# Fewer helpers on GpSimd, and 512 moving columns in four linears of a two-block transformer kernel

## The chip, the cores and the metric

The kernel runs on one core of a Trainium2 chip. TensorE (PE) does matrix products, VectorE (DVE) and ScalarE (ACT) elementwise work, GpSimd (POOL) a little of the same, and SyncE (SP) issues most DMAs. The metric is the device time of one execution in microseconds, as a median of several runs.

## The reference

Two transformer blocks on 256 tokens of width 1024, everything in float32, about 150 MB of weights. Cut to the linears and norms that matter here:

```python
# first block; 16 meta tokens in front, so 272 rows
proj  = rms_norm(h, g0) @ w_in                      # 1024 -> 5128
mixed = (sigmoid(g_a) * (o_a @ w_o_fox) + sigmoid(g_b) * (o_b @ w_o_sb)) @ w_out
h = h + rms_norm(mixed, g1)
u = causal_depthwise_conv(rms_norm(h, g2) @ w_up)   # 1024 -> 5632, 3 taps
ffn = (gelu(u_gate) * u_val) @ w_down               # 2816 -> 1024
h = h + rms_norm(ffn, g3)
# second block, 256 tokens
proj = rms_norm(x, g_mix) @ w_in_2                  # 1024 -> 8192: qa ka va qr kr vr gr ga gr
x = x + (sigmoid(ga) * (ya @ w_branch_diff) + sigmoid(gr) * (yr @ w_branch_ret)) @ w_out_2
x = x + square(relu(rms_norm(x, g_mlp) @ w_ff1)) @ w_ff2
x = x + sigmoid(rms_norm(x, g_ple) @ w_ple_gate) * (p @ w_ple)
return rms_norm(x, g_final)
```

`o_a` and `o_b` are two attentions of the first block; `ya` (differential attention) and `yr` (retention) belong to the second.

## The kernel before

**Precision.** Every large product is made of three matmuls. A weight slab `w` (up to 1024 rows by 256 columns, as 8 chunks of 128 rows) is split into a high part `whi`, which ScalarE writes by a copy (`Weights.split_unit`, L87), and a low part `wlo` = `w` - `whi`, by a subtraction (`Weights.finish`, L96). Activations have high and low parts too (`xh` and `xl`, `fh` and `fl`). The three products are high by high, high by low and low by high.

**Weights.** The object `ws` walks a list of slabs, `plan`, in the order in which the program uses them. SyncE loads half slabs ("units", 128 partitions by 1024 elements, tile `raw`, five buffers). `ws.start(n)` splits the next unit or units on ScalarE, at most two slabs ahead; `ws.finish()` issues the subtractions that belong to them and the next loads; `ws.next()` hands out the next slab and splits it on the spot if that has not been done. Before, `finish` puts a subtraction on GpSimd in two cases: when it is called as `finish(True)` (in the residual of the first block, at the end of w_down, and in the first va wave), and as every fourth one while `ws.share` is 4, that is, during w_up. That makes 17 of 284.

**Two forms of linear.** `feat_tile` (L320 to L323) holds the weights still and moves the activations: the result has features on the partitions. `token_tile` (L333 to L336) holds 128 tokens still and moves the weights: the result has tokens on the partitions. Four linears have the second form: w_down, va and vr of the second block, and ple_gate. They take slabs of 256 columns and 256 moving columns.

**Order of the work.** The program is written in the order in which each engine executes it. Between two tiles of a linear stands `period()`: it starts the next units' high parts on ScalarE, lets the evacuation of the tile before go on a step (`side.evac`), runs a step of side work such as attention (`side.tick`), and ends with the low parts (`ws.finish`). Evacuations are generators, one step at each `yield`. A linear may begin with a wave: three tiles share each chunk, while the chunk's activation is still being made by `make(k)`.

**The places touched.** In w_up, `ev_conv` evacuates a tile of 258 columns: VectorE multiplies it by the reciprocal root (`ur`, L302), applies the taps of the convolution (`cv`, two instructions at L308, one on ScalarE), and after each second tile makes the gated product. In w_down, `ev_down` copies a tile to `rawt` and sums its squares (`ssf`); the last tile's rows are scaled with a reciprocal root (`down_rstd`, `down_scale`), transposed (`turn_raw`) and added to the residual `R`, from which ScalarE makes `xh` and VectorE `xl` for the second block's first linear, va. This is called the join below. Its square sums (`squares`, `mix_sums`) are folded from eight chunks to two on GpSimd and summed by TensorE against a column of ones. `ev_mix` makes the `xl` of the gated mix, six of its eight low parts on GpSimd.

Of the kernel before, what the change touches and what calls it, by code (L numbers as in the profile page):

```python
# [27 lines left out]
DOWN = ((0, 6), (6, 8), (14, 8))  # L28
# [141 lines left out]
def two_blocks_kernel(  # L170
# [42 lines left out]
    for c in range(0, D, 256):  # L213
        for k, nk in DOWN:
            cols(w_down[0], c, 256, k, nk)
    all_cols(w_in_2, 2 * D, D)
# [3 lines left out]
    all_cols(w_in_2, 3 * D, 5 * D)  # L220
# [7 lines left out]
    all_cols(w_ple_gate[0], 0, D)  # L228
# [188 lines left out]

    def tp_tile(tag, n):
# [6 lines left out]
    def period(gen=None, finish=True):  # L425
        ws.start()
# [4 lines left out]
        if finish:  # L431
# [8 lines left out]

    def token_tiles(slabs, X):
        for _ in range(slabs):
            W = ws.next()
            for t in range(2):
                yield lambda ps, k, nk, part=None, W=W, t=t: token_tile(
                    ps, X, W, k, k, t, k == 0, k == nk - 1)

    def linear(tiles, nk, evac, wave=0, make=None, sums=None, after=None, settle=9, hold=0, pump=(2, 4)):
# [31 lines left out]
        for f in tiles:  # L480
# [6 lines left out]
            j += 1  # L487

# [348 lines left out]
    def ev_mix(ps, j):  # L837
# [5 lines left out]
        (G if j < 6 else V).tensor_tensor(xl[:, j, 0:NQ], t, f32(xh[:, j, 0:NQ]), ALU.subtract)  # L843
# [40 lines left out]
    def residual(sums, after, toks, off, n, gout, gnext, fill):  # L884
# [5 lines left out]
        ws.finish(True)  # L890
# [21 lines left out]
        def make(k):  # L912
# [11 lines left out]
            if k in (5, 7):  # L924
# [95 lines left out]
    for c in range(4):  # L1020
        pss = [mm(), mm()]
        for k0, nk in DOWN:
            W = ws.next()
# [4 lines left out]
            for t in range(2):  # L1028
                for k in range(nk):
                    token_tile(pss[t], FX, W, k0 + k, k, t, k0 + k == 0, k0 + k == KF1 - 1)  # L1030
                if c < 3 or not last:
                    period(ev_down(pss[t], c, t) if last else None)
                    continue
                side.flush()
                next(ev_down(pss[t], c, t))
                if t == 0:
                    down_scale(0, down_rstd(0))
# [45 lines left out]
    def ev_va(ps, c, t):  # L1083
        A.activation(va[:, t, c * 256:(c + 1) * 256], ps[:, 0:256], AF.Identity, scale=r3[:, t:t + 1])
# [3 lines left out]
    wave = [[mm(), mm()], [mm(), mm()]]  # L1088
# [3 lines left out]
    for t in range(2):  # L1092
# [3 lines left out]
        for k in range(KD):  # L1096
# [49 lines left out]
    def ev_tokens(dst):  # L1146
        def go(ps, j):
            c, t = divmod(j, 2)
            A.activation(dst[:, t, c * 256:(c + 1) * 256], ps[:, 0:256], AF.Identity,
                         scale=r3[:, t:t + 1])  # L1150
# [136 lines left out]
    W = None  # L1287
    for j in range(4):
        c, t = divmod(j + 4, 2)
        W = W if t else ws.next()  # L1290
        ps = mm()
        for k in range(KD):
            token_tile(ps, X3, W, k, k, t, k == 0, k == KD - 1)
        if j == 0:
            ws.start()
            ws.finish()
            mix_sums(1)
            mix_rstd(1)
# [211 lines left out]
```

## Time and profile before

| | before |
|---|---|
| median of 3 runs | 939.78 us (938.76, 939.78, 940.41) |
| the profiled execution | 937.62 us; its span 935.8 us |
| TensorE busy | 909.7 us, 97%, 7457 matmuls |
| weight loads (PEld) busy | 884.8 us, 95% |
| VectorE busy | 647.0 us, 69% |
| ScalarE busy | 522.5 us, 56% |
| GpSimd busy | 88.1 us, 9%, 75 instructions |
| DMA | 154.73 MB, mean 165 GB/s |

The span is the stretch from the first to the last instruction in the trace; the execution's own time is 1.8 us longer. Stages, by the trace: w_up runs from about 240 to 362 us, w_down from 362 to 431 us, the join and the first va wave from 431 to about 459 us, ple_gate at the end. PEclk is the clock granted to TensorE as a share of full speed.

### The profile page before, as it was taken

Reading aid. Unit: us, or ns where it says so; the run is one execution under the profiler, and the core shown is the slowest. Engines: PE = TensorE matmul, PEld = TensorE weight load, DVE = VectorE, ACT = ScalarE, POOL = GpSimd, SP = SyncE. Lnnn points to the kernel's source line nnn. Section 1 sums busy time; section 2 is a strip of 40 time slices with the busy share of each in tenths; the row PEclk is TensorE's granted clock in tenths of the full one; section 3 lists DMA queues with packets and bytes.
Section 4 is the critical chain, followed back from the end, with each engine's and each line's share of the span. In section 5 each row is a group of like instructions: output and inputs, shape, how many; then the busy total and the mean of one; then the engine's idle time right before and its main releaser. Section 6 shows DMA issues by size and latency. Waiting matters only on the chain.

```text
span 935.8 us, 18318 instructions
## 1 busy us (share of the span) xinstructions
PE 909.7 (97%) x7457; PEld 884.8 (95%) x7457; DVE 647.0 (69%) x1150; ACT 522.5 (56%) x948; POOL 88.1 (9%) x75
## 2 busy tenths in 40 slices
PE   8999999999999999999899999999999999999996
PEld 5999989998999999898899999999999999999996
DVE  5667666667899999536667765577787666655546
ACT  5535566656666666546556564446645566544435
POOL 5021100032422222003200000000000000000000
PEclk8999999999999999999999999999999999999998
DMA  8554343664355555663555465455465666565631
GB/s 268 169 147 137 112 130 100 202 212 136 113 164 179 180 173 163 208 197 113 180 164 153 147 195 167 139 166 191 143 200 179 185 197 189 172 203 180 197 120 45
DMA packets 149715, 154.73 MB, mean 165 GB/s; under 512 B 5260, under 2 KB 145808, under 8 KB 149632
## 3 DMA queue, kind: packets, MB, share of 16 engines
q1 hardware_dynamic: 147904, 149.56, 51.7%
q0 software_dynamic: 1376, 3.36, 1.1%
q8 instruction: 58, 0.95, 0.4%
q10 hardware_dynamic: 352, 0.66, 0.2%
q14 instruction: 25, 0.20, 0.1%
HBM read 152.50 MB, written 1.05 MB: 164 GB/s over the span
## 4 chain that ended last, share of the span: by engine, by line
PE 77%; DVE 16%; ACT 3%; issue 2%; DMA 1%; POOL 0%; SPq 0%; DVEq 0%; ACTq 0%
PE mm L320 19%; PE mm L323 19%; PE mm L321 19%; DVE cv L308 5%; DVE wlo L96 4%; PE mm L336 4%; PE mm L333 4%; PE mm L334 4%; DVE ur L302 2%; DVE cv L302 1%; PE at L678 1%; DMA raw<-in_w_in_dram 1%; PE at L1164 1%; ACT whi L87 1%; DVE u L989 1%
## 5 line engine op out<-in xcount | busy, mean ns | idle before, releaser
L96 DVE TENSOR_TENSOR wlo<-raw,whi 128x1024 fp32r<-128x1024 f32 (+1 forms) x267 | 324.4, 1223 | 98.5 <-ACT whi L87 97.8
L87 ACT ACTIVATE whi<-raw 128x1024 fp32r<-128x1024 f32 (+1 forms) x284 | 292.0, 1047 | 172.5 <-PE mm L323 87.9
L323 PE MATMUL mm<-xl,whi 128*128 128x258 f32 (+2 forms) x1256 | 351.1, 283 | 1.3 <-DVE xl L308 1.3
L320 PE MATMUL mm<-xh,whi 128*128 128x258 f32 (+3 forms) x1192 | 341.5, 287 | 1.9 <-ACT xh L542 1.9
L321 PE MATMUL mm<-xh,wlo 128*128 128x258 f32 (+3 forms) x1192 | 337.0, 283 | 0.3 <-DVE wlo L96 0.3
L323 PEld LDWEIGHTS mm<-xl,whi 128*128 128x128 f32 x1256 | 235.4, 189 | 2.0 <-DVE xl L308 1.7
L320 PEld LDWEIGHTS mm<-xh,whi 128*128 128x128 f32 (+1 forms) x1192 | 224.7, 189 | 5.3 <-issue 2.3
L321 PEld LDWEIGHTS mm<-xh,wlo 128*128 128x128 f32 (+1 forms) x1192 | 224.8, 189 | 1.5 <-DVE wlo L96 1.2
L320 PE MATMUL mm<-u,whi 128*128 128x256 f32 (+1 forms) x704 | 198.3, 282 | 0.0
L321 PE MATMUL mm<-u,wlo 128*128 128x256 f32 (+1 forms) x704 | 197.0, 280 | 0.0
L323 PE MATMUL mm<-u,whi 128*128 128x256 f32 (+1 forms) x576 | 162.6, 282 | 0.0
L321 PEld LDWEIGHTS mm<-u,wlo 128*128 128x128 f32 x704 | 133.0, 189 | 0.0
L320 PEld LDWEIGHTS mm<-u,whi 128*128 128x128 f32 x704 | 132.5, 188 | 0.0
L323 PEld LDWEIGHTS mm<-u,whi 128*128 128x128 f32 x576 | 108.4, 188 | 0.0
L333 PE MATMUL mm<-whi,u 128*128 128x256 f32 x240 | 68.2, 284 | 2.4 <-ACT whi L87 2.4
L334 PE MATMUL mm<-wlo,u 128*128 128x256 f32 x240 | 68.2, 284 | 1.5 <-DVE wlo L96 0.9
L336 PE MATMUL mm<-whi,u 128*128 128x256 f32 x240 | 68.0, 283 | 0.0
L308 DVE SCALAR_TENSOR_TENSOR cv<-ur,gc,cv 128x256 f32<-128x256 f32 x88 | 66.2, 755 | 1.6
L96 POOL TENSOR_TENSOR wlo<-raw,whi 128x1024 fp32r<-128x1024 f32 x17 | 40.8, 2405 | 174.8 <-ACT whi L87 93.0
L333 PEld LDWEIGHTS mm<-whi,u 128*128 128x128 f32 x240 | 45.8, 191 | 2.6 <-ACT whi L87 2.6
L334 PEld LDWEIGHTS mm<-wlo,u 128*128 128x128 f32 x240 | 46.0, 192 | 1.9 <-DVE wlo L96 1.1
L302 DVE TENSOR_TENSOR u<-mm,rb 128x256 f32<-128x256 f32 (+2 forms) x68 | 28.8, 423 | 27.1 <-PE mm L323 26.6
(337 smaller groups left out, 1058.9 us busy)
## 6 DMA issues: line engine op xcount, KB each, us to landing
raw<-in_w_in_dram SPq DMA_DIRECT2D x102, 512.0 KB, 3.8
raw<-in_w_ff_dram SPq DMA_DIRECT2D x64, 512.0 KB, 3.9
raw<-in_w_up_dram SPq DMA_DIRECT2D x44, 512.0 KB, 3.5
raw<-in_w_out_dram SPq DMA_DIRECT2D x16, 512.0 KB, 4.5
raw<-in_w_down_dram SPq DMA_DIRECT2D x16, 512.0 KB, 4.5
raw<-in_w_branch_diff_dram SPq DMA_DIRECT2D x8, 512.0 KB, 3.4
raw<-in_w_branch_ret_dram SPq DMA_DIRECT2D x8, 512.0 KB, 3.9
raw<-in_w_ple_gate_dram SPq DMA_DIRECT2D x8, 512.0 KB, 3.9
```

Of the source, the lines that this page charges most:

```text
L87: self.nc.scalar.activation(hi[:, a:b], w, AF.Copy)
L96: eng.tensor_tensor(lo, w, f32(hi), ALU.subtract)
L302: V.tensor_tensor(o, a, b, ALU.mult)
L308: V.scalar_tensor_tensor(out=o, in0=a, scalar=s, in1=b, op0=op0, op1=op1)
L320: T.matmul(ps, sh, mh, start=first, stop=False)
L321: T.matmul(ps, sl, mh, start=False, stop=False)
L323: T.matmul(ps, sh, ml, start=False, stop=last)
L333: T.matmul(ps[:, 0:256], hi, W[0][:, k, :], start=first, stop=False)
L334: T.matmul(ps[:, 0:256], hi, W[1][:, k, :], start=False, stop=False)
L336: T.matmul(ps[:, 0:256], lo, W[0][:, k, :], start=False, stop=last)
L678: T.matmul(S[i][0:kk.stop - kk.start, o], k[r, c, kk], q[r, c, qq], start=False, stop=kk.stop == 272, skip_group_check=True)
L989: V.tensor_tensor(fl[f // 8][:, f % 8, :], t, f32(fh[f // 8][:, f % 8, :]), ALU.subtract)
```

## The change

1. `finish` puts every low part on VectorE; `ws.share` goes. The calls `finish(True)` go too: in the residual one unit is split by `ws.start(1)` and finished inside the loop that follows; at the end of w_down and in the va wave the units are split one or two at a time.
2. The six `xl` of `ev_mix` move from GpSimd to VectorE. The folds of the squares go, and TensorE sums eight chunks in place of two.
3. w_down, va, vr and ple_gate take slabs of four chunks (in w_down the last of two) by 512 columns, and each matmul moves 512 columns into a whole PSUM bank. A new function `wide` runs such a linear; the first va wave holds two tiles in place of four, and ple_gate begins with a wave of two tiles. Evacuations take 512 columns at a time, in ple_gate as two halves.
4. The last two slabs of w_down are used tile by tile (all of token tile 0, then all of tile 1), and the reciprocal root's sum is one addition.

```diff
-DOWN = ((0, 6), (6, 8), (14, 8))
+DOWN = ((0, 4), (4, 4), (8, 4), (12, 4), (16, 4), (20, 2))
...
-    def finish(self, idle=False):
+    def finish(self):
         for lo, w, hi in self.todo:
-            self.lows += 1
-            idle = idle or self.share and self.lows % self.share == 0
-            eng = self.nc.gpsimd if idle else self.nc.vector
-            eng.tensor_tensor(lo, w, f32(hi), ALU.subtract)
+            self.nc.vector.tensor_tensor(lo, w, f32(hi), ALU.subtract)
...
-            T.matmul(ps[:, 0:256], hi, W[0][:, k, :], start=first, stop=False)
+            T.matmul(ps, hi, W[0][:, k, :], start=first, stop=False)
...
+    def wide(groups, ks, X, evac):
+
+        kall = sum(nk for _, nk in ks)
+        for c in groups:
+            pss = [mm(), mm()]
+            for k0, nk in ks:
+                W = ws.next()
+                last = k0 + nk == kall
+                for t in range(2):
+                    for k in range(nk):
+                        token_tile(pss[t], X, W, k0 + k, k, t, k0 + k == 0, k0 + k == kall - 1)
+                    period(evac(pss[t], c, t) if last else None)
...
-        (G if j < 6 else V).tensor_tensor(xl[:, j, 0:NQ], t, f32(xh[:, j, 0:NQ]), ALU.subtract)
+        V.tensor_tensor(xl[:, j, 0:NQ], t, f32(xh[:, j, 0:NQ]), ALU.subtract)
...
         y = sums.rstd()
-        ws.finish(True)
+        ws.start(1)
...
-            if k in (5, 7):
+            if k in (1, 5, 7):
                 ws.finish()
...
-    for c in range(4):
-        pss = [mm(), mm()]
-        for k0, nk in DOWN:
-            W = ws.next()
-            last = k0 + nk == KF1
-            if c == 3 and last:
-                ws.start(2)
-                ws.finish(True)
...
+    wide((0,), DOWN, FX, ev_down)
+    pss = [mm(), mm()]
+    for k0, nk in DOWN[:-2]:
+        W = ws.next()
+        for t in range(2):
+            for k in range(nk):
+                token_tile(pss[t], FX, W, k0 + k, k, t, k0 + k == 0, False)
+            period()
+    Ws = [ws.next(), ws.next()]
+    for t in range(2):
+        for (k0, nk), W in zip(DOWN[-2:], Ws):
+            for k in range(nk):
+                token_tile(pss[t], FX, W, k0 + k, k, t, False, k0 + k == KF1 - 1)
+        ws.start(1)
+        side.flush()
+        next(ev_down(pss[t], 1, t))
+        ws.finish()
+        if t == 0:
+            down_scale(0, down_rstd(0))
...
-        if i:
-            for n in (4, 2):
-                G.tensor_tensor(sqs[:, t, 0:n, :], sqs[:, t, 0:n, :], sqs[:, t, n:2 * n, :], ALU.add)
...
-        for i in range(2):
-            T.matmul(ps[:, 0:1], sqs[:, t, i, :], ones[:, 0:1], start=i == 0, stop=i == 1)
+        for i in range(KD):
+            T.matmul(ps[:, 0:1], sqs[:, t, i, :], ones[:, 0:1], start=i == 0, stop=i == KD - 1)
...
     W = [ws.next(), ws.next()]
-    wave = [[mm(), mm()], [mm(), mm()]]
+    wave = [mm(), mm()]
...
-            elif k in (2, 4):
+            elif k in (2, 5):
                 ws.start(1)
-            elif k in (3, 5):
-                ws.finish(True)
-            for part in range(2):
-                for c in range(2):
-                    token_tile(wave[t][c], X3, W[c], k, k, t, k == 0, k == KD - 1, part)
+            elif k in (4, 7):
+                ws.finish()
+            token_tile(wave[t], X3, W[k // 4], k, k % 4, t, k == 0, k == KD - 1)
...
-    linear(token_tiles(4, X3), KD, ev_tokens(vr))
+    wide((0, 1), KS, X3, ev_tokens(vr))
...
-    linear(token_tiles(4, chunks(xh2, xl2)), KD, ev_ple_gate, wave=3, settle=0, after=gate_rstd())
+    XP = chunks(xh2, xl2)
+    W = [ws.next(), ws.next()]
+    pss = [mm(), mm()]
+    for k in range(KD):
+        for t in range(2):
+            token_tile(pss[t], XP, W[k // 4], k, k % 4, t, k == 0, k == KD - 1)
+        if k in (2, 4):
+            ws.pump(1)
+        if k == KD - 2:
+            side.flush()
+    side.first = side.step([gate_rstd()])
+    for t in range(2):
+        side.evacs.append((0, ev_ple_gate(pss[t], 0, t)))
+    ws.pump(2)
+    side.first = side.step(side.first)
+    wide((1,), KS, XP, ev_ple_gate)
```

The first place is VectorE in w_up, four tiles before the change: `wlo` is a low part of a weight unit, `ur` and `cv` are the scaled tile and the tile after the taps, and the `u_` tiles hold the GELU's gate and the gated product.

```order
L302 TENSOR_TENSOR ur<-mm,rb_2689 128x258
L308 SCALAR_TENSOR_TENSOR cv<-ur,gc,cv 128x256 x2
L302 TENSOR_TENSOR cv<-cv 128x256
L96 TENSOR_TENSOR wlo<-raw,whi 128x1024
L302 TENSOR_TENSOR ur<-mm,rb_2689 128x258
L308 SCALAR_TENSOR_TENSOR cv<-ur,gc,cv 128x256 x2
L302 TENSOR_TENSOR cv<-cv 128x256
L989 TENSOR_TENSOR u_2686<-cv,u_2683 128x256
L96 TENSOR_TENSOR wlo<-raw,whi 128x1024
L302 TENSOR_TENSOR ur<-mm,rb_2689 128x258
L308 SCALAR_TENSOR_TENSOR cv<-ur,gc,cv 128x256 x2
```

The third tile has no `wlo` on this engine. The same engine and place after the change:

```order
L304 TENSOR_TENSOR ur<-mm,rb_2686 128x258
L310 SCALAR_TENSOR_TENSOR cv<-ur,gc,cv 128x256 x2
L304 TENSOR_TENSOR cv<-cv 128x256
L1001 TENSOR_TENSOR u_2683<-cv,u_2680 128x256
L93 TENSOR_TENSOR wlo<-raw,whi 128x1024
L304 TENSOR_TENSOR ur<-mm,rb_2686 128x258
L310 SCALAR_TENSOR_TENSOR cv<-ur,gc,cv 128x256 x2
L1001 TENSOR_TENSOR u_2683<-cv,u_2680 128x256
L93 TENSOR_TENSOR wlo<-raw,whi 128x1024
L304 TENSOR_TENSOR ur<-mm,rb_2686 128x258
L310 SCALAR_TENSOR_TENSOR cv<-ur,gc,cv 128x256 x2
L93 TENSOR_TENSOR wlo<-raw,whi 128x1024
```

Each tile now has its `wlo` on VectorE; nothing else was added there.

The second place is ScalarE at the join, before the change. `u_4437` is `rawt`, the copied result of w_down; `sq,ssf` is the square with its sum; `ny` is a step of the reciprocal root; the `xh` with `R` and `gc` is the first of va.

```order
L87 ACTIVATE whi<-raw 128x1024 x5
L1000 ACTIVATE u_4437<-mm 128x256
L1001 ACTIVATE sq,ssf<-mm 128x256
L359 ACTIVATE ny<-sf,epsc 128x1
L362 ACTIVATE ny<-ny 128x1
L1014 ACTIVATE u_4437<-u_4437,nr 128x256 x2
L1000 ACTIVATE u_4437<-mm 128x256
L1001 ACTIVATE sq,ssf<-mm 128x256
L1062 ACTIVATE xh<-R,gc 128x128 x3
```

All five `whi` stand ahead of the evacuations. The same engine and place after the change:

```order
L87 ACTIVATE whi<-raw 128x1024
L1010 ACTIVATE u_4437<-mm 128x512
L1011 ACTIVATE sq,ssf<-mm 128x512
L361 ACTIVATE ny<-sf,epsc 128x1
L364 ACTIVATE ny<-ny 128x1
L1023 ACTIVATE u_4437<-u_4437,nr 128x256 x2
L87 ACTIVATE whi<-raw 128x1024
L1010 ACTIVATE u_4437<-mm 128x512
L1011 ACTIVATE sq,ssf<-mm 128x512
L87 ACTIVATE whi<-raw 128x1024 x2
L1072 ACTIVATE xh<-R,gc 128x128 x3
```

One `whi` now stands between the two last evacuations, and two stand behind the last one and ahead of the first `xh`.

The third place is VectorE at the join, before the change; `sf`, `nh`, `nt` and `nr` are the reciprocal root's steps, and `at` is the bank with the transposed result.

```order
L96 TENSOR_TENSOR wlo<-raw,whi 128x1024 x6
L1007 TENSOR_REDUCE sf<-ssf 128x1
L360 TENSOR_SCALAR nh<-sf 128x1
L308 SCALAR_TENSOR_TENSOR nt<-ny,nh 128x1
L308 SCALAR_TENSOR_TENSOR nr<-nt,ny 128x1
L1016 TENSOR_SCALAR u_4437<-u_4437,nr 128x256 x2
L308 SCALAR_TENSOR_TENSOR R<-at,gc,R 128x128 x3
L308 SCALAR_TENSOR_TENSOR xl<-R,gc,xh 128x128
```

No `wlo` of VectorE stands between the scaling and the first `R`. The same place after the change:

```order
L93 TENSOR_TENSOR wlo<-raw,whi 128x1024
L307 TENSOR_TENSOR sf<-ssf 128x1
L362 TENSOR_SCALAR nh<-sf 128x1
L310 SCALAR_TENSOR_TENSOR nt<-ny,nh 128x1
L310 SCALAR_TENSOR_TENSOR nr<-nt,ny 128x1
L1025 TENSOR_SCALAR u_4437<-u_4437,nr 128x256 x2
L93 TENSOR_TENSOR wlo<-raw,whi 128x1024 x3
L310 SCALAR_TENSOR_TENSOR R<-at,gc,R 128x128 x3
L310 SCALAR_TENSOR_TENSOR xl<-R,gc,xh 128x128
```

Three `wlo` now stand there.

## Rows read from the trace of the kernel before

**Rows 1.** The page, busy us of an engine (share of the span) and instructions

```profile
PE 909.7 (97%) x7457; PEld 884.8 (95%) x7457; DVE 647.0 (69%) x1150; ACT 522.5 (56%) x948; POOL 88.1 (9%) x75
```

**Rows 2.** TensorE's waits, 150 to 530 us: us in all, times, longest

```profile
PE mm L333 <- ACT whi L87: 2.4, 1, 2.4
PE at L392 <- DVE acc L400: 1.6, 1, 1.6
```

**Rows 3.** Windows: us, busy PE PEld DVE ACT POOL, PEclk, DMA share, GB/s

```profile
295.00:305.00 10.00, 10.00 (x86) 10.00 (x85) 9.89 (x15) 6.36 (x11) 2.39 (x1) 1.00 0.59 192
375.00:380.00 5.00, 3.41 (x18) 3.22 (x19) 4.31 (x5) 4.02 (x5) 0.00 (x0) 0.77 0.35 111
450.00:455.00 5.00, 5.00 (x34) 5.00 (x33) 2.36 (x2) 2.13 (x3) 2.01 (x2) 0.72 0.09 29
```

**Rows 4.** ScalarE's timeline, evacuations of w_down: start us, busy us, [idle before <- releaser]

```profile
412.72 0.38 ACT L1000 ACTIVATE u<-mm 128x256 f32<-128x256 f32 x1 [0.82 <-PE mm L336]
...
428.33 0.38 ACT L1000 ACTIVATE u<-mm 128x256 f32<-128x256 f32 x1 [0.82 <-PE mm L336]
```

**Rows 5.** TensorE's timeline, filler matmuls of the residual

```profile
229.13 0.39 PE L323 MATMUL at<-u,u 128*128 128x512 f32 x1
...
231.21 0.40 PE L323 MATMUL mm<-u,u 128*128 128x512 f32 x1
```

**Rows 6.** VectorE's timeline in w_up

```profile
290.58 0.42 DVE L302 TENSOR_TENSOR ur<-mm,rb 128x258 f32<-128x258 f32 x1
...
296.69 3.00 DVE L308 SCALAR_TENSOR_TENSOR cv<-ur,gc,cv 128x256 f32<-128x256 f32 x2
...
301.19 1.22 DVE L96 TENSOR_TENSOR wlo<-raw,whi 128x1024 fp32r<-128x1024 f32 x1
302.33 0.42 DVE L302 TENSOR_TENSOR ur<-mm,rb 128x258 f32<-128x258 f32 x1
302.67 0.99 DVE L308 SCALAR_TENSOR_TENSOR cv<-ur,gc,cv 128x256 f32<-128x256 f32 x2
...
369.92 0.42 DVE L302 TENSOR_TENSOR ur<-mm,rb 128x258 f32<-128x258 f32 x1
```

**Rows 7.** TensorE's timeline, the first matmul of w_down

```profile
362.25 0.28 PE L333 MATMUL mm<-whi,u 128*128 128x256 f32 x1
```

**Rows 8.** ScalarE's timeline, the table load in w_down

```profile
373.31 1.28 ACT L1019 ACT_TABLE_LOAD   x1
```

**Rows 9.** TensorE's timeline at the join and in the va wave

```profile
433.69 0.39 PE L333 MATMUL mm<-whi,xh 128*128 128x256 f32 x1 [0.44 <-ACT xh L1062]
...
447.94 0.38 PE L336 MATMUL mm<-whi,xl 128*128 128x256 f32 x1 [2.74 <-DVE xl L308]
...
454.78 0.50 PE L1078 MATMUL at<-ones,u 128*128 128x1 f32 x4
455.14 0.37 PE L333 MATMUL mm<-whi,xh 128*128 128x256 f32 x1
```

**Rows 10.** The page, costliest groups: a high part of a weight unit

```profile
L87 ACT ACTIVATE whi<-raw 128x1024 fp32r<-128x1024 f32 (+1 forms) x284 | 292.0, 1047 | 172.5 <-PE mm L323 87.9
```

**Rows 11.** VectorE's timeline at the join

```profile
429.87 1.59 DVE L308 SCALAR_TENSOR_TENSOR nt<-ny,nh 128x1 f32<-128x1 f32 x1 [0.41 <-ACT ny L362]
...
432.85 0.35 DVE L308 SCALAR_TENSOR_TENSOR R<-at,gc,R 128x128 f32<-128x128 f32 x1 [0.55 <-PE at L1052]
```

**Rows 12.** VectorE's timeline in the residual of the first block

```profile
219.59 3.42 DVE L96 TENSOR_TENSOR wlo<-raw,whi 128x1024 fp32r<-128x1024 f32 x1
```

**Rows 13.** TensorE's timeline in the wave at the head of w_up

```profile
240.39 0.39 PE L323 MATMUL mm<-xl,whi 128*128 128x258 f32 x1 [1.12 <-DVE xl L308]
```

**Rows 14.** ScalarE's timeline, the last sigmoid

```profile
926.78 0.47 ACT L1433 ACTIVATE t<-mm,nr 128x256 f32<-128x256 f32 x1 [0.44 <-PE mm L336]
```

More of the change, by code (lines that the diff above doesn't have):

```diff
@@ L19 @@
 P = 128
+KS = ((0, 4), (4, 4))
 D = 1024
@@ L212, in two_blocks_kernel, with wide_cols @@
         cols(w_up[0], FF1 + i * 256, 256)
[L213 to L216, printed above, removed]
+    def wide_cols(w, c0, width, ks=((0, 4), (4, 4))):
+        for c in range(c0, c0 + width, 512):
+            for k, nk in ks:
+                cols(w, c, 512, k, nk)
+    wide_cols(w_down[0], 0, D, DOWN)
+    wide_cols(w_in_2, 2 * D, D)
     for c in range(0, D, 256):
@@ L219, in two_blocks_kernel @@
         cols(w_in_2, D + c, 256)
-    all_cols(w_in_2, 3 * D, 5 * D)
+    all_cols(w_in_2, 3 * D, D)
+    wide_cols(w_in_2, 4 * D, D)
+    all_cols(w_in_2, 5 * D, 3 * D)
     all_cols(w_br_diff[0], 0, D)
@@ L332, in token_tile @@
         if part != 1:
-            T.matmul(ps[:, 0:256], hi, W[0][:, k, :], start=first, stop=False)
-            T.matmul(ps[:, 0:256], hi, W[1][:, k, :], start=False, stop=False)
+            T.matmul(ps, hi, W[0][:, k, :], start=first, stop=False)
+            T.matmul(ps, hi, W[1][:, k, :], start=False, stop=False)
         if part != 0:
-            T.matmul(ps[:, 0:256], lo, W[0][:, k, :], start=False, stop=last)
+            T.matmul(ps, lo, W[0][:, k, :], start=False, stop=last)
     def chunks(hi, lo):
@@ L416, in bcast, with wide_tile @@
                      start=True, stop=True)
+    def wide_tile(tag):
+        return tp.tile([P, 512], F32, tag="w", name=tag, bufs=1)
     def tp_tile(tag, n):
@@ L423, in tp_tile, with period @@
         return tp.tile([P, 418], F32, tag="b", name=tag, bufs=7)[:, :n]
-    def period(gen=None, finish=True):
-        ws.start()
+    def period(gen=None, split=True):
+        if split:
+            ws.start()
         side.evac()
@@ L430, in period @@
         side.tick()
-        if finish:
+        if split:
             ws.finish()
@@ L1006, in down_rstd @@
         ss = sp.tile([P, 1], F32, tag="sf", name="sf")
-        V.tensor_reduce(out=ss, in_=ssf[:, 4 * t:4 * t + 4], axis=AX.X, op=ALU.add)
+        add(ss, ssf[:, 2 * t:2 * t + 1], ssf[:, 2 * t + 1:2 * t + 2])
         return rstd_narrow(ss, P, 1, 1.0 / D)
@@ L1019, in two_blocks_kernel @@
     A.preload_act_table_set(EXP_LN)
-    for c in range(4):
-        pss = [mm(), mm()]
-        for k0, nk in DOWN:
-            W = ws.next()
-            last = k0 + nk == KF1
-            if c == 3 and last:
-                ws.start(2)
-                ws.finish(True)
[L1028 to L1037, printed above, removed]
+    wide((0,), DOWN, FX, ev_down)
[17 more added lines that the diff above has]
+            down_scale(0, down_rstd(0))
     hi = unit("xh", F32R, (P, KD, L1))
@@ L1122, in two_blocks_kernel @@
             if t == 1 and k == 5:
-                next(ev_va(wave[0][0], 0, 0))
-                next(ev_va(wave[0][1], 1, 0))
+                next(ev_va(wave[0], 0, 0))
     Rx = R[:, :, 2:258]
@@ L1146, in ev_tokens, with go @@
     def ev_tokens(dst):
[L1147 to L1150, printed above, removed]
+        def go(ps, c, t):
+            A.activation(dst[:, t, c * 512:(c + 1) * 512], ps, AF.Identity, scale=r3[:, t:t + 1])
             yield
@@ L1285, in mix_rows @@
         yield
[L1287 to L1298, printed above, removed]
-            next(ev_va(wave[1][0], 0, 1))
-            next(ev_va(wave[1][1], 1, 1))
-        if j == 1:
-            side.add(mix_rows())
-        period(ev_va(ps, c, t))
+    pss = [mm(), mm()]
+    for i in range(2):
+        W = ws.next()
+        for t in range(2):
+            for k in range(4):
+                token_tile(pss[t], X3, W, 4 * i + k, k, t, i == 0 and k == 0, i == 1 and k == 3)
+            if i == 0 and t == 0:
+                ws.start()
+                ws.finish()
+                mix_sums(1)
+                mix_rstd(1)
+                next(ev_va(wave[1], 0, 1))
+            if i == 0 and t == 1:
+                side.add(mix_rows())
+            period(ev_va(pss[t], 1, t) if i else None)
     side.flush()
```

55 lines of the change are left out of this document (27 added, 28 removed).

## The prediction, made before the changed kernel had run

> **What bounds the kernel now.** The page first: TensorE is busy for 97% of the span, VectorE for 69% [rows 1]. So nearly every microsecond is matmul time, and a change can win in two ways: by a cheaper matmul, or at the few places where TensorE stands. The list of TensorE's waits for 150 to 530 us gives, beside an `xl` that comes in part 3, 2.4 us for ScalarE's `whi` and 1.6 us for VectorE's `acc` [rows 2]. The stretches show what stands behind them: VectorE is busy 9.89 of 10 us inside w_up; and behind the two longest waits, the `whi` and the `xl`, the granted clock falls to 0.77 and 0.72 of a 5 us stretch, that is, to the 1.2 GHz level for part of it [rows 3]. After that I read the VectorE timeline in w_up and the chain at the join from w_down to the second block's first linear.
>
> The profiled execution took 937.62 us (span 935.8, 1.8 around it); the median of the runs is 939.78, 2.16 above. I sum against the profiled execution and put the sum under the median.
>
> **1. Wide matmuls.** The four linears have 528 (w_down) and three times 192 matmuls of 256 columns, 1104 together; 552 of 512 columns take their place. Price before: the first evacuations of two successive w_down groups stand 15.61 us apart with 132 matmuls between, 0.1183 us each [rows 4]. Price after: the kernel already has 24 matmuls of 512 columns, in the filler of the residual; nine starts from 229.13 to 231.21 are 0.2311 us apart [rows 5]. A pair thus goes from 0.2366 to 0.2311, and 552 times 0.0055 is 3.0 us. The other end is zero, since the filler ran while few transfers did, and a wide matmul beside the weight stream may cost two narrow ones; a loss I exclude, as it would need idle time between matmuls that the filler doesn't show. I take 2.2 us, nearer the measured end. By rows, then, halving the instructions and weight loads is worth 2%, not half.
>
> The Trainium skill, "TensorE: Matmul & The Clock Gate", section "Back-to-back issue gap", says that in a stream of weight loads and matmuls a 512-column matmul is sustained at about 131 ns. By it the sum would be some 58 us lower (an estimate: 552 times 0.105 us). The 231 ns of [rows 5] decide against it here; it returns below as a rival.
>
> **2. GpSimd's low parts in w_up: the largest term.** Of four low parts three run on VectorE and one on GpSimd. While GpSimd runs its one, VectorE's pair of `cv` takes 3.00 us instead of 0.99: it loses 2.01 us to spare a `wlo` that costs it 1.14 (1.22 long, next start 1.14 on) [rows 6]. Four tiles take VectorE 11.75 us (290.58 to 302.33 [rows 6]); TensorE needs 96 matmuls of 258 columns, 11.45 us at the price per column of part 1. So VectorE falls behind: its last `ur` starts at 369.92 [rows 6], 7.7 us after TensorE began w_down at 362.25 [rows 7]. Without GpSimd four tiles cost 11.75 - 2.01 + 1.14 = 10.88 us, 0.6 under TensorE's time and 0.87 under before; over ten such rounds that is 8.7 us, more than the lag. VectorE will be level with TensorE well before the end.
>
> What the lag costs: the last `ur` gates the last `cv`, then ScalarE's table load (1.28 us at 373.31 [rows 8]), then the third slab's `whi`, for which TensorE stands, and a fallen clock follows. From 362.25 to the evacuation at 412.72 TensorE has 372 matmuls, 44.0 us; 50.5 passed. So 6.4 us are lost there. With the last `ur` 7 us earlier, the table load is over by about 367 and the third slab is split by 370; TensorE wants it after two wide slabs, at 362.25 + 48 x 0.231 = 373.3. Nothing is late next: the slab's buffers and data were free before. I take -6.3; the bounds are -6.4 and -4.0 (idle gone in part, clock still falling).
>
> **3. The join of w_down and the next linear: a loss.** Before, both slabs of the first va wave are split ahead (`start(2)`, half on GpSimd). After, `ws.next()` splits the second slab only when it is asked for, so on ScalarE two `whi` stand behind the evacuation of the last tile and ahead of the first `xh`, and on VectorE three `wlo` stand ahead of the first `R` (both orders are shown with the change). Let T be the end of w_down's last matmul; before, 24 matmuls after 428.33, T = 431.1, and the first va matmul came at 433.69 [rows 9], 2.6 after T, of which transposes fill 1.1: idle 1.5. After: evacuation of 512 columns, two operations and an accumulator read, about 1.2 (an estimate from 0.38 for 256 columns [rows 4]); two `whi` of 1.05 [rows 10], T+3.2; the last `wlo`, T+4.5; from the first `R` to the first matmul 0.84 as before (432.85 [rows 11] to 433.69), T+5.4. Idle 4.3 us: +2.8. Bounds: +1 (the evacuation quicker, `whi` earlier), +4.
>
> The square sums lose GpSimd's folding: two products with a one-column moving operand take 0.36 us (454.78 to the next matmul at 455.14 [rows 9]); eight take 1.44, twice: +2.2. In return GpSimd no longer stalls the small `nt`, 1.59 us for one column [rows 11], and the 2.74 us that TensorE stood at 447.94 [rows 9] go, less 0.2 for a `wlo` put in the loop: -2.5. The clock fell here before for some 16 matmuls; after a longer stand it falls too: +0.2. Sum of the join: +2.7.
>
> **4. Smaller edits.** Residual: GpSimd's `wlo` at 219.5 held VectorE's for 3.42 us [rows 12], and the 1.6 us for `acc` [rows 2] came of it: -1.6. In its place VectorE gets a `wlo` inside the loop that makes `xh`, where TensorE already stands 1.12 us at the end [rows 13]: +0.6, between 0 and 1.7. Mix evacuation: six `xl` of 258 columns come to VectorE, each under the 0.42 of the same form in [rows 6]; the read that frees the third bank of the w_out wave comes just in time now and moves to about 0.6 late: +0.6, between 0 and 1.4. Tail: the last tile holds 512 columns, so one more 256-half of multiply, add and square follows the last matmul's sigmoid at 926.78 [rows 14]: +1.1, between 0.4 and 1.6. The vr linear keeps its eight periods; its evacuations lie beside matmuls.
>
> **Sum:** -2.2 - 6.3 + 2.7 - 1.6 + 0.6 + 0.6 + 1.1 = -5.1 us: 932.5 for the profiled execution, 934.7 for the median, 0.54% faster.
>
> **Rivals.** (a) *w_down's stand stays.* If the last evacuations wait for something other than VectorE's lag (ScalarE's table load, the order of its queue), only one GpSimd stall of 2.0 less one `wlo` comes off, -1.2 instead of -6.3: 939.8, no change. For it: the named releaser is ScalarE [rows 2]. Against: ScalarE is busy 6.36 of 10 us there [rows 3], and the lag of the last `ur` covers it all. 11 in 100. (b) *Slower: the clock stays down through the va wave.* The 4.3 us stand is longer than the 2.7 before, and the wave that follows has TensorE waiting for VectorE chunk by chunk. Its 48 wide matmuls at half clock lose some 0.2 us each, 9.6 in place of the 1.7 in my sum: 942.6. It decides from about 44 matmuls on. Against it: before, the clock was back within one stretch of 5 us [rows 3]. 6 in 100. (c) *The weight load sets the pitch.* If 0.118 is the load's and not the columns', a wide matmul costs as much as a narrow one: -65 us, 874. TensorE's loads are busy for 95% [rows 1]; against it the 0.231 of [rows 5]. 1 in 100. The rule of the Trainium skill cited above is of this kind; by it the time would be some 880 (an estimate).
>
> **How the numbers follow.** My case holds 82 in 100; its own range adds the bounds above, 931 to 938. What this measurement can tell from no change is 0.2%, 1.9 us: under 937.9 is faster, over 941.7 slower. Of the 82, three fall within 0.2%; of (a) nine are no change, one each side; of (b) five slower, one no change; (c) is faster. Faster 81, same 13, slower 6. The range is 930.8 to 938.4; it reaches toward (a) and leaves out most of (a), (b) and (c).
>
> **What would show it.** Right: no TensorE wait between 360 and 385 and a granted clock of 1.0 there; the last `ur` within 2 us of w_up's last matmul; wide matmuls 0.231 apart; a new stand of about 4 us for ScalarE's `xh` (or VectorE's `R`) at the join, with `whi` and `wlo` in front of it; eight products of 1.4 us in each square sum. Wrong: VectorE still full in w_up; a pitch of 0.236 beside transfers; a join without the stand, or one whose slow clock lasts.

## The result and the profile after

The changed kernel takes 932.83 us (median of 4 runs, 932.24 to 934.22) against 939.34 (median of 4, 938.76 to 940.41). The ratio is 0.9932, interval 0.9914 to 0.9949: 0.68% or, by the medians, 6.5 us faster. Forecast were 934.7 us and 5.1 us less. The profiled execution took 932.24 us with a span of 930.4, so the two traces differ by 5.4 us; the remaining 1.1 us lies in which executions were profiled, since that of before was 1.7 under its median and that of after 0.6.

The page of the changed kernel, busy time by engine, answers to [rows 1]:

```profile
PE 908.1 (98%) x6929; PEld 860.2 (92%) x6929; DVE 636.2 (68%) x1173; ACT 521.3 (56%) x928; POOL 37.0 (4%) x48
```

TensorE executes 528 matmuls fewer and is busy only 1.6 us less, so a wide matmul costs nearly what the two narrow ones in its place did. VectorE took over most of GpSimd's work and is busy 10.8 us less: its instructions in w_up no longer run beside GpSimd's low parts.

TensorE's waits, 150 to 530 us (us in all, times, longest), answer to [rows 2]:

```profile
PE mm L335 <- ACT xh L1072: 4.4, 1, 4.4
PE mm L325 <- DVE xl L310: 2.2, 3, 1.1
PE mm L322 <- DVE t L304: 0.6, 1, 0.6
```

The waits for `whi` (2.4), `acc` (1.6) and the long `xl` (2.7) are gone. A new one of 4.4 us leads the list, the waits for `xl` in w_up's wave have grown from 1.3 to 2.2, and one of 0.6 for `t` is new.

Windows of the changed kernel (us, busy PE PEld DVE ACT POOL, PEclk, DMA share, GB/s) answer to [rows 3]:

```profile
295.00:305.00 10.00, 10.00 (x86) 10.00 (x85) 9.86 (x20) 6.94 (x12) 0.00 (x0) 1.00 0.61 184
375.00:380.00 5.00, 5.00 (x23) 4.03 (x22) 2.26 (x3) 1.48 (x3) 0.00 (x0) 1.00 0.73 222
425.00:430.00 5.00, 1.41 (x3) 1.16 (x4) 4.19 (x10) 2.80 (x8) 0.00 (x0) 0.73 0.72 212
430.00:435.00 5.00, 5.00 (x17) 3.92 (x16) 3.61 (x14) 3.71 (x10) 0.00 (x0) 0.59 0.32 104
435.00:440.00 5.00, 5.00 (x35) 4.43 (x34) 2.73 (x10) 2.63 (x6) 0.00 (x0) 1.00 0.01 3
```

In w_down (375 to 380) the clock is at full speed now, and TensorE does not stand. At the join it stands, and the clock falls to the 1.2 GHz level for part of ten microseconds. A trap is in the first row: VectorE is as full in w_up as before (9.86 against 9.89 of 10 us), which the prediction had named as a sign of being wrong. Yet it does 20 instructions there in place of 15; a busy share does not say whether an engine keeps up.

VectorE's timeline shows that it does (start us, busy us); the rows answer to [rows 6]:

```profile
292.57 0.42 DVE L304 TENSOR_TENSOR ur<-mm,rb 128x258 f32<-128x258 f32 x1
292.91 1.00 DVE L310 SCALAR_TENSOR_TENSOR cv<-ur,gc,cv 128x256 f32<-128x256 f32 x2
...
303.45 0.42 DVE L304 TENSOR_TENSOR ur<-mm,rb 128x258 f32<-128x258 f32 x1
...
330.78 0.43 DVE L304 TENSOR_TENSOR ur<-mm,rb 128x258 f32<-128x258 f32 x1 [0.37 <-PE mm L325]
...
362.42 0.42 DVE L304 TENSOR_TENSOR ur<-mm,rb 128x258 f32<-128x258 f32 x1
```

Four tiles take 10.88 us (292.57 to 303.45) in place of 11.75, to the digit the forecast figure, and each pair of `cv` takes 1.0. At 330.78 VectorE waits for TensorE for the first time behind the wave: the lag is worked off. The last `ur` starts at 362.42. TensorE's first matmul of w_down is at 362.18, so the lag is 0.2 us, where it was 7.7.

The join on TensorE, ScalarE and VectorE, three fences that answer to [rows 9] and [rows 11]. TensorE first:

```profile
422.89 0.40 PE L338 MATMUL mm<-whi,u 128*128 128x512 f32 x1
423.13 1.03 PE L1062 MATMUL at<-tab,u 128*128 128x128 f32 x8
428.59 0.80 PE L335 MATMUL mm<-whi,xh 128*128 128x512 f32 x1 [4.43 <-ACT xh L1072]
429.18 0.63 PE L336 MATMUL mm<-wlo,xh 128*128 128x512 f32 x1
```

ScalarE:

```profile
423.34 0.59 ACT L1010 ACTIVATE u<-mm 128x512 f32<-128x512 f32 x1
423.82 0.59 ACT L1011 ACTIVATE sq<-mm 128x512 f32<-128x512 f32 x1
424.30 0.20 ACT L1011 ACTIVATION_READ_ACCUMULATOR sq<-mm 128x1 f32 x1
424.39 2.00 ACT L87 ACTIVATE whi<-raw 128x1024 fp32r<-128x1024 f32 x2
428.14 0.98 ACT L1072 ACTIVATE xh<-R,gc 128x128 fp32r<-128x128 f32 x3 [1.75 <-DVE R L310]
```

VectorE:

```profile
423.46 1.23 DVE L93 TENSOR_TENSOR wlo<-raw,whi 128x1024 fp32r<-128x1024 f32 x1 [1.27 <-ACT whi L87]
425.48 2.36 DVE L93 TENSOR_TENSOR wlo<-raw,whi 128x1024 fp32r<-128x1024 f32 x2 [0.79 <-ACT whi L87]
427.76 0.86 DVE L310 SCALAR_TENSOR_TENSOR R<-at,gc,R 128x128 f32<-128x128 f32 x3
```

Read them as a chain: w_down ends at 423.1, ScalarE copies and squares until 424.4, then splits two units until 426.3. VectorE follows with two `wlo` until 427.76, and only then come `R`, `xh` and the first matmul of va at 428.59, 5.5 us after the end of w_down. The list of waits names `xh`. What holds it is `R`, and what stands ahead of `R` are two weight units that are wanted four chunks later; the run that moves them (e6) tests this.

The time between matched points of TensorE's timeline, summed from those timelines:

| stage | before | after | difference | forecast |
|---|---|---|---|---|
| head, to w_in's last part | 111.15 | 110.01 | -1.1 | 0 |
| to the residual's filler (mix, w_out) | 113.32 | 112.30 | -1.0 | -1.0 |
| the filler | 6.97 | 6.96 | 0.0 | 0 |
| w_up with its wave | 130.81 | 132.91 | +2.1 | +0.6 |
| w_down | 68.73 | 60.95 | -7.8 | -7.4 |
| join, va | 33.21 | 35.54 | +2.3 | +2.3 |
| to vr; vr; to ple_gate | 438.80 | 438.28 | -0.5 | -0.4 |
| ple_gate, tail | 32.81 | 33.45 | +0.6 | +0.7 |

(The forecast spreads its 2.2 us for the wide matmuls over the four linears by their counts.) The head holds nothing that was changed. In the ten traces of this study it ends between 109.8 and 113.5 us whatever the kernel, and it begins with waits for the first loads, so its 1.1 us are scatter.

### The profile page after: what moved, and what is told of

It is laid out like the page before. It is cut to its first block, busy times and chain, and to the rows that moved or that the text cites. A ratio compares the mean times of both kernels' runs of the same rounds, so it can differ in the third digit from the quotient of the medians.

```text
span 930.4 us, 17216 instructions
## 1 busy us (share of the span) xinstructions
PE 908.1 (98%) x6929; PEld 860.2 (92%) x6929; DVE 636.2 (68%) x1173; ACT 521.3 (56%) x928; POOL 37.0 (4%) x48
## 4 chain that ended last, share of the span: by engine, by line
PE 91%; DVE 4%; ACT 2%; issue 1%; DMA 1%; POOL 0%; SPq 0%; DVEq 0%; ACTq 0%
PE mm L322 24%; PE mm L325 23%; PE mm L323 23%; PE mm L335 4%; PE mm L338 4%; PE mm L336 4%; DVE wlo L93 1%; PE at L690 1%; PE at L1166 1%; DMA raw<-in_w_in_dram 1%; ACT whi L87 1%; PE at L757 1%; PE at L768 1%; PE at L721 0%; DVE t L304 0%
## 5 line engine op out<-in xcount | busy, mean ns | idle before, releaser
L93 DVE TENSOR_TENSOR wlo<-raw,whi 128x1024 fp32r<-128x1024 f32 (+1 forms) x284 | 343.0, 1217 | 100.0 <-ACT whi L87 99.5
L335 PE MATMUL mm<-whi,u 128*128 128x512 f32 x120 | 47.4, 395 | 0.0
L336 PE MATMUL mm<-wlo,u 128*128 128x512 f32 x120 | 47.2, 393 | 0.0
L338 PE MATMUL mm<-whi,u 128*128 128x512 f32 x120 | 47.0, 392 | 0.0
L310 DVE SCALAR_TENSOR_TENSOR cv<-ur,gc,cv 128x256 f32<-128x256 f32 x88 | 42.0, 480 | 1.6
L989 ACT ACTIVATE cv<-ur,gc 128x256 f32<-128x256 f32 x44 | 26.2, 599 | 17.0 <-DVE ur L304 16.9
L304 DVE TENSOR_TENSOR t<-t 128x256 f32<-128x256 f32 x32 | 13.6, 425 | 27.0 <-ACT t L1385 27.0
L335 PE MATMUL mm<-whi,xh 128*128 128x512 f32 x64 | 27.2, 425 | 4.4 <-ACT xh L1072 4.4
```

What stands on the lines that cost most here:

```text
L93: self.nc.vector.tensor_tensor(lo, w, f32(hi), ALU.subtract)
L304: V.tensor_tensor(o, a, b, ALU.mult)
L310: V.scalar_tensor_tensor(out=o, in0=a, scalar=s, in1=b, op0=op0, op1=op1)
L335: T.matmul(ps, hi, W[0][:, k, :], start=first, stop=False)
L336: T.matmul(ps, hi, W[1][:, k, :], start=False, stop=False)
L338: T.matmul(ps, lo, W[0][:, k, :], start=False, stop=last)
```

## The experiments

The kernel before took 938.96 us (17 runs) beside e1 to e4 and 937.55 us (11 runs) beside e5 to e8, so kernels are compared by their ratio to it; the changed kernel's, measured beside neither, is 0.9932. Each interval is about 0.2% to each side, 1.7 us, and a difference between two such ratios is less certain still, by some 2.4 us (an estimate: 1.7 times the root of two). Smaller differences are read from the traces, and a trace shows one execution only.

**The GpSimd share alone (e1).** One line out of the kernel before:

```diff
-    ws.share = 4
     linear(feat_tiles(KF1, X2, 0, NQ), KD, ev_conv, wave=3, make=make, sums=s1,
```

> The kernel before with one part of the change alone: in w_up all low parts go to VectorE, the rest (256-column slabs, GpSimd in the residual, at the join and for the folds) stays. My theory (the lag of VectorE behind w_up makes the stand in w_down): the last ur comes within 2 us of w_up's last matmul, TensorE has no wait for whi between 362 and 385 us, the clock there stays at 1.0, and the time falls by 6.3 us, to about 933.0. Rival (the new slabs of w_down took the stand away, VectorE's lag only a part): the wait for whi in w_down stays, and the time falls by about 1.2 us, to 938.

Measured: 933.12 us, ratio 0.9934 (0.9916 to 0.9952). VectorE's last `ur` and, in the second fence, the window in w_down:

```profile
364.03 0.42 DVE L302 TENSOR_TENSOR ur<-mm,rb 128x258 f32<-128x258 f32 x1
```

```profile
375.00:380.00 5.00, 5.00 (x45) 5.00 (x44) 2.36 (x2) 2.12 (x6) 0.00 (x0) 1.00 1.04 354
```

w_down begins at 363.79 here, 0.2 us before that `ur`, and the clock in the window is at 1.00. TensorE's longest waits, 150 to 530 us, hold no `whi` any more:

```profile
PE mm L336 <- DVE xl L308: 3.1, 2, 2.7
PE at L392 <- DVE acc L400: 1.6, 1, 1.6
PE mm L323 <- DVE xl L308: 1.3, 2, 1.1
```

The two waits for `wlo` in w_down (0.9 and 0.6) have gone as well; the rest of the list is as before. From the start of w_down to the next linear with features on the partitions it is 95.59 us in place of 101.94: 6.35 less, where 6.3 was forecast. Rival (a) has fallen, since the old slabs lose the stand too. And this one line is worth as much as the whole change: all its other parts together come to nothing that can be measured.

**The share put back (e3).** The changed kernel, with `self.lows` counted again and

```diff
-            self.nc.vector.tensor_tensor(lo, w, f32(hi), ALU.subtract)
+            self.lows += 1
+            idle = self.share and self.lows % self.share == 0
+            eng = self.nc.gpsimd if idle else self.nc.vector
+            eng.tensor_tensor(lo, w, f32(hi), ALU.subtract)
...
+    ws.share = 4
     linear(feat_tiles(KF1, X2, 0, NQ), KD, ev_conv, wave=3, make=make, sums=s1,
            after=next_rstd(s1, NQ, [(rb2, 1.0)], box))
+    ws.share = 0
```

> The changed kernel with every fourth low part of w_up on GpSimd again, the rest as changed. My theory: VectorE's cv beside GpSimd's wlo takes 3 us again, the last ur starts about 7 us after w_down's first matmul, TensorE stands for whi or wlo of w_down's third slab, the clock falls there, and the time rises by 5 us (3 to 7), to about 938. Rival (the new slabs alone remove the stand): 1 us more at most, 934.

Measured: 939.15 us, ratio 1.0007 (0.9993 to 1.002), 7 us more than the changed kernel: the whole gain is lost. GpSimd's `wlo` in w_up and, in the second fence, VectorE's pairs of `cv` beside it and behind it, and the last `ur`:

```profile
295.51 2.40 POOL L97 TENSOR_TENSOR wlo<-raw,whi 128x1024 fp32r<-128x1024 f32 x1 [9.37 <-DVE wlo L97]
```

```profile
295.70 3.01 DVE L314 SCALAR_TENSOR_TENSOR cv<-ur,gc,cv 128x256 f32<-128x256 f32 x2
299.30 1.00 DVE L314 SCALAR_TENSOR_TENSOR cv<-ur,gc,cv 128x256 f32<-128x256 f32 x2
...
369.56 0.42 DVE L308 TENSOR_TENSOR ur<-mm,rb 128x258 f32<-128x258 f32 x1
```

ScalarE behind that `ur` and, in the second fence, TensorE at w_down's third slab:

```profile
372.95 1.28 ACT L1034 ACT_TABLE_LOAD   x1
374.25 2.00 ACT L88 ACTIVATE whi<-raw 128x1024 fp32r<-128x1024 f32 x2
```

```profile
375.36 0.50 PE L339 MATMUL mm<-whi,u 128*128 128x512 f32 x1 [2.62 <-ACT whi L88]
376.62 0.80 PE L340 MATMUL mm<-wlo,u 128*128 128x512 f32 x1 [0.76 <-DVE wlo L97]
```

And the window after it:

```profile
375.00:380.00 5.00, 3.88 (x9) 2.90 (x10) 4.66 (x5) 4.09 (x5) 0.00 (x0) 0.59 0.42 129
```

w_down begins at 361.31, so the last `ur` is 8.3 us late; the pair of `cv` takes 3.01 again, the table load and the `whi` come late behind them, TensorE stands 2.6 and 0.8 us, and the clock falls. From both sides the stand thus hangs on GpSimd's low parts in w_up, not on the slabs.

**Two narrow matmuls for each wide one (e2).** In the changed kernel's `token_tile`:

```diff
-            T.matmul(ps, hi, W[0][:, k, :], start=first, stop=False)
...
+        for x, w, i in ((hi, W[0], 0), (hi, W[1], 1), (lo, W[0], 2)):
+            step = 512 if first and i == 0 else 256
+            for c in range(0, 512, step):
+                T.matmul(ps[:, c:c + step], x, w[:, k, c:c + step], start=first and i == 0,
+                         stop=last and i == 2 and c == 256)
```

> The changed kernel with each matmul of 512 moving columns issued as two of 256 into the halves of the same bank (only the first product of each tile, 16 in all, stays whole); slabs, order and everything else stay. My theory: 536 pairs cost 0.0055 us each more, 2.9 us, so about 935.7. Rival 1 (the wide ones lose beside the weight stream what they save): no change, 932.8. Rival 2 (the load sets the pitch): some 65 us more.

Measured: 934.48 us, ratio 0.9958 (0.9944 to 0.9972). TensorE's timeline at the start and the end of w_down:

```profile
362.96 0.39 PE L337 MATMUL mm<-whi,u 128*128 128x512 f32 x1
...
425.45 0.27 PE L1062 MATMUL at<-tab,u 128*128 128x128 f32 x1
```

w_down takes 62.49 us here and 60.95 with wide matmuls. That is 1.54 us over 260 pairs, 0.0059 us each, beside the weight stream: 536 pairs make 3.2. By the ratios e2 takes 2.4 us more than the changed kernel, which alone would not exclude rival 1; the trace of w_down does, and rival 2 falls by either. So the filler's 0.0055 holds under load, and the value taken, 2.2, was too low: the price lies at the upper bound of 3.0 or just above it. The changed kernel's wide matmuls in w_down are 0.231 us apart (60.95 us over 264). The Trainium skill, "TensorE: Matmul & The Clock Gate", section "Back-to-back issue gap", gives about 131 ns for a 512-column matmul in a stream of weight loads and matmuls. This trace disagrees: by that figure e2 would have lost some 27 us in this stage (an estimate: 260 times 0.105), where 1.5 were measured.

**Six of eight products left out of each square sum (e4).**

```diff
-        for i in range(KD):
-            T.matmul(ps[:, 0:1], sqs[:, t, i, :], ones[:, 0:1], start=i == 0, stop=i == KD - 1)
+        for i in range(2):
+            T.matmul(ps[:, 0:1], sqs[:, t, i, :], ones[:, 0:1], start=i == 0, stop=i == 1)
```

> The changed kernel with two products in each square sum at the join in place of eight; the squares of the other six chunks are left out of the reciprocal root. My theory: each product of one moving column costs TensorE 0.18 us on the path, twelve fewer take 2.2 us off, 930.6. Rival (TensorE waits for VectorE in that wave anyway): under 0.7 us, 932.2 or more.

Measured: 930.36 us, ratio 0.991 (0.9894 to 0.9925), some 2.1 us less than the changed kernel. In the changed kernel's trace the first sum is 16 records long:

```profile
438.32 1.84 PE L1085 MATMUL at<-ones,u 128*128 128x1 f32 x16
440.02 0.48 PE L335 MATMUL mm<-whi,xh 128*128 128x512 f32 x1
```

1.70 us to the next matmul, against 0.36 with two products: 1.34 more for each sum, 2.7 for both. From w_down's start to the linear after va e4 takes 92.68 us and the changed kernel 96.49: 3.8 less, these 2.7 and about 1.1 that its shorter stretch of slow clock gave back (7 wide matmuls in place of 13). The price stands on the path, and the rival falls; the forecast's 2.2 was a little low.

**The residual's unit earlier (e5).**

```diff
-        y = sums.rstd()
         ws.start(1)
+        y = sums.rstd()
+        ws.finish()
         fill(1)
...
-            if k in (1, 5, 7):
+            if k in (5, 7):
                 ws.finish()
```

> The changed kernel, in the first block's residual: the extra unit is split ahead of the reciprocal root and its low part is made right behind it, so no wlo stands in the chunks 1 to 3 of w_up's wave. My theory (that wlo on VectorE is what lengthens the wave): the waits for xl before chunks 2 and 3 (0.32 and 0.73 us in the changed kernel) shrink to the one of 0.17 that the kernel before had, and the time falls by 0.9 us, to 931.9; more, up to 2.5, if the clock falls there in many runs. Rival (VectorE's R and t, held by GpSimd's additions, set the wave anyway): no change, 932.8.

Measured: 929.93 us, ratio 0.9913 (0.9893 to 0.9934), 1.8 us under the changed kernel's ratio, a difference that the two intervals don't tell apart from none. In the trace, of TensorE's waits, the one in w_up's wave is 1.3 us in all, as in the kernel before (0.17 and 1.12):

```profile
PE mm L325 <- DVE xl L310: 1.3, 2, 1.1
```

w_up with its wave takes 130.06 us in place of 132.91. Only 0.9 of these 2.9 us are the waits. Most of the rest shows in the window 240 to 245 us, here the changed kernel's:

```profile
240.00:245.00 5.00, 5.00 (x36) 5.00 (x36) 2.81 (x7) 0.46 (x2) 0.85 (x1) 0.71 0.63 204
```

The kernel of e4 has the same residual:

```profile
240.00:245.00 5.00, 3.88 (x37) 3.68 (x36) 4.36 (x8) 2.33 (x6) 2.11 (x2) 1.00 0.36 105
```

With the same instructions and the same three waits (2.2 us in all), the clock fell behind them in the traces of the changed kernel and of e7, and did not in those of e2, e4 and e6, where w_up took 131.4 to 131.5 us. In e3, with a fourth wait (2.9 us in all), it did not fall either. So about 1.5 us of the changed kernel's w_up come and go from one execution to the next. In the four traces with the shorter waits (before, e1, e5, e8) the clock stayed at 1.00 there; that it does so in every execution is not shown.

**The units of the join moved (e6).**

```diff
-        ws.start(1)
+        ws.start(2 - t)
         side.flush()
         next(ev_down(pss[t], 1, t))
...
-    W = [ws.next(), ws.next()]
+    W = [ws.next()]
...
+                if k == 0:
+                    ws.start(1)
                 if k == 1:
+                    ws.finish()
+                    W.append(ws.next())
                     y = down_rstd(1)
```

> The changed kernel with the units of the join moved: both units of va's first slab are split at the end of token tile 0, one unit of the second slab at the end of tile 1, and its last one inside the loop behind the first chunk; no whi stands any more between the last evacuation and the first xh. My theory (the two whi and the two wlo in front of the first R are the 4.4 us stand): the first matmul of va comes 2.4 us after w_down's last one in place of 5.5, one wlo of 1.2 us returns as a wait inside the wave at most, and the time falls by 2 to 3 us, to about 930.3. Rival (VectorE's whole work in the wave sets its end, so the stand only moves): under 0.7 us, 932.3.

Measured: 931.09 us, ratio 0.9921 (0.9903 to 0.9938), only 1.0 us under the changed kernel's: between theory and rival, and inside the intervals. In the trace, w_down's start to the linear after va takes 94.97 us against 96.49, 1.5 less. TensorE's timeline:

```profile
425.60 0.51 PE L335 MATMUL mm<-whi,xh 128*128 128x512 f32 x1 [1.28 <-ACT xh L1072]
...
429.70 0.50 PE L338 MATMUL mm<-whi,xl 128*128 128x512 f32 x1 [1.84 <-DVE xl L310]
```

VectorE's:

```profile
426.83 1.23 DVE L93 TENSOR_TENSOR wlo<-raw,whi 128x1024 fp32r<-128x1024 f32 x1 [0.37 <-ACT whi L87]
427.97 0.15 DVE L307 TENSOR_TENSOR sf<-ssf 128x1 f32<-128x1 f32 x1
...
429.31 0.34 DVE L310 SCALAR_TENSOR_TENSOR xl<-R,gc,xh 128x128 fp32r<-128x128 f32 x1
```

And the window 430 to 435 us:

```profile
430.00:435.00 5.00, 4.92 (x19) 3.72 (x19) 3.63 (x14) 3.40 (x10) 0.00 (x0) 0.66 0.21 72
```

The first matmul of va came as forecast (425.60, against the end of w_down's last at 423.3: 2.3 us), and the stand of 4.4 fell to 1.3. But the moved `wlo`, with the second tile's reciprocal root behind it, keeps the third chunk's `xl` back: a new wait of 1.84. The clock fell behind that one as it had behind the other. I had counted the new wait at 1.2 at most, and not the clock.

**The folds on VectorE (e7).**

```diff
+        if i:
+            for n in (4, 2):
+                V.tensor_tensor(sqs[:, t, 0:n, :], sqs[:, t, 0:n, :], sqs[:, t, n:2 * n, :], ALU.add)
...
-        for i in range(KD):
+        for i in range(2):
...
```

> The changed kernel with the squares folded from eight chunks to two on VectorE (512 and 256 columns, behind the last xl of each token tile) and two products in each sum. My theory: the folds lie in VectorE's wait for the transposes of the second tile (1.3 us there) and beside matmuls, so the whole price of the twelve products comes back, 2.5 us by the run that left them out: 930.4. Rival (the fold of the first tile delays the second tile's first R by its 1 us): 931.5.

Measured: 930.45 us, ratio 0.9922 (0.9901 to 0.9943). TensorE's sum of the first tile is short again:

```profile
439.77 0.50 PE L1088 MATMUL at<-ones,u 128*128 128x1 f32 x4
440.13 0.48 PE L335 MATMUL mm<-whi,xh 128*128 128x512 f32 x1
```

and the fold lies on VectorE just ahead of the second tile's `R`:

```profile
435.53 1.15 DVE L1083 TENSOR_TENSOR u<-u 128x512 f32<-128x512 f32 x2 [0.17 <-ACT u L1079]
436.75 0.87 DVE L310 SCALAR_TENSOR_TENSOR R<-at,gc,R 128x128 f32<-128x128 f32 x3
```

From w_down's start to the linear after va it is 94.36 us against 96.49, 2.1 less. Its theory said 2.5 and its rival 1.3, and the execution times (0.9 less by the ratio, 2.4 by the medians) don't tell them apart. This trace was one in which the clock fell in w_up.

**The three together (e8).**

> The changed kernel with the three edits together: the residual's unit earlier, the units of the join moved, the folds on VectorE. If their places are independent, the gains add: 0.9 + 2.5 + 2.4 = 5.8 us, 927.0. Rival (they share VectorE's time at the join, so the folds or the moved wlo return as waits): 929 to 930.

Measured: 926.8 us (median of 4, 925.87 to 927.7), ratio 0.9876 (0.9854 to 0.9898): the fastest version here, 1.24% under the kernel before and 5.3 us under the changed kernel's ratio; among the faster versions it alone has an interval that lies clear of the changed kernel's. That is near the 5.8 of gains that add, but the 5.8 counted 2.5 for e6 and 2.4 for e7, where their ratios gave 1.0 and 0.9; the gains as measured one by one add to 3.7. The windows at the join:

```profile
425.00:430.00 5.00, 3.09 (x12) 1.73 (x11) 4.23 (x15) 3.48 (x11) 0.00 (x0) 1.00 0.58 192
430.00:435.00 5.00, 5.00 (x29) 4.12 (x28) 4.56 (x15) 3.43 (x8) 0.00 (x0) 1.00 0.02 3
```

Here the clock stayed at full speed through the join, although TensorE stands at the same two places as long as in e6 (1.3 us for `xh`, 1.8 for `xl`) and another 0.7 later. w_down to the linear after va takes 92.07 us against 96.49, 4.4 less, where e6 and e7 had 1.5 and 2.1; the clock that stayed up is part of the rest, so the agreement with 5.8 is in part luck.

## Why the prediction was right

The time lies inside the range, and the sign and the size hold. The largest term holds in size and mechanism. Others were mis-sized by up to 1.5 us, and in the sum these errors nearly cancel: against the forecast by stage, w_up took 1.5 more, w_down 0.4 less, and the head, where nothing was changed, 1.1 less. That the traces differ by 5.4 us where 5.1 were forecast is therefore partly luck.

- **w_up and w_down, -6.3.** Shown from both sides: -6.35 us in that stretch when only the share is taken out (e1), the whole gain lost when it is put back (e3). The mechanism has all its links in the traces: GpSimd's `wlo` beside VectorE's `cv` (3.0 against 1.0 us), the late `ur`, the late table load and third slab, the stand, the fallen clock. One reading was incomplete: 11.75 against 11.45 us in four tiles adds 0.3 us a round, 3.0 in ten, not the whole 7.7. Most of the lag is there at the start. At w_up's fifth tile `ur` starts 6.0 us behind TensorE's last matmul of that tile before and 4.0 in the changed kernel; from there it grows to 7.8 before, and at 10.88 us a round it shrinks to 0.2.
- **Wide matmuls, -2.2.** 0.0059 us a pair beside the stream (e2), so about -3.3 for the 552; the term was undersized by 1 us because I discounted the filler's figure for a load that then cost nothing.
- **The join, +2.7.** The first va matmul was forecast at T+5.4 and came at T+5.5; the idle time, put at 4.3, came to 4.4. Inside the term errors partly cancel, which is luck: the sums cost 2.7 and not 2.2, and the fallen clock took 2.6 us (13 wide matmuls of 0.43 in place of 0.23) where it had taken 1.6 before (16 narrow ones), +1.0 and not +0.2. Against that, the wave's waits for `xl` went whole, 3.1 us in two waits (the list of e1, whose join is that of before, has them) and not the 2.5 of the longest alone. These parts add up to some +2.8 when 0.6 comes off for the wide matmuls; the stage took 2.3 more, so 0.5 us stays unexplained. Rival (b) did not come about: the clock was back by 435 us.
- **Residual and mix, -1.0.** Came to -1.0: the wait for `acc` is gone, and the read that frees the w_out wave's bank is 0.59 us late (0.6 forecast).
- **w_up's wave, +0.6.** This is the term that was mis-sized. The waits grew by 0.9, within the bounds, but behind them the clock fell in some executions for another 1.5 us, and I had looked for that at the join alone. The rest of w_up gained some 0.8 us when the share went (130.01 in e1 against 130.81). In e5's trace both the added waits and the fall are gone.
- **Tail, +1.1.** With the wide gain taken off, +0.6 in the stage against +0.7.

What moved the median 1.4 us beyond the forecast is less than the interval (1.6 us to each side), and the traces don't explain it: without the head they differ by 4.3 us.

Why the clock falls behind some stands of a given length and not behind others stays open. e6 and e8 at the join, and the five traces of w_up's wave, show the difference with no edit between the stand and the fall that would explain it.

## What to carry to other kernels

A helper engine that makes its neighbour slower is paid for by the neighbour: compare the neighbour's instruction with and without company before sharing work, and look for the cost where the lag lands (here in the next stage, behind a table load), not where it arises. When work units are taken ahead of a loop, take only those that the loop's first steps need (1.5 us in e6's trace). And a stand on the bounding engine can cost more than its length: behind the changed kernel's 4.4 us at the join came 2.6 us of slow clock. Whether it is cheaper to break it up is not settled here: e8 stood 3.1 us in two parts and kept its clock, e6 did the same and lost it.

## What the runs showed of the hardware

- VectorE's pair of `cv` (128x256) takes 1.0 us alone and 3.0 beside GpSimd's subtraction of 128x1024 (2.4 us), in e3 as in the kernel before; in e1 and the changed kernel no such pair behind the wave takes more than 1.0: GpSimd's work costs its neighbour nearly twice the 1.14 us that it spares it.
- A 512-column product of float32r operands starts every 0.231 us (60.95 us over 264 in w_down) and two of 256 columns every 0.237 (62.49 over 264, e2): halving the instructions and loads is worth 2.5%.
- A sum product of plain float32 with one moving column stands as two records in the trace and costs TensorE about 0.2 us (1.70 for eight), nearly as much as a float32r product with 512 columns.
- The clock's fall is not a fixed price of a stand: after the same three waits in w_up's wave (2.2 us in all) it fell in two traces of five, to 0.71 and 0.66 of a 5 us stretch.
